# A hybrid attention and RWKV-7 block on one Trainium2 core: the second half's first RWKV head pair placed after the first half's attention in the program text

## The chip, the cores and the metric

The kernel runs on one core of a Trainium2 chip. What counts is the device time of one execution in microseconds, from the first instruction to the last; for the kernel before it is given as the median of three runs. The engines are called by the names that the profile uses: PE is TensorE's matmul stream, PEld its weight loads, DVE is VectorE, ACT is ScalarE, POOL is GpSimd and SP is SyncE, which issues most of the DMAs.

## The reference, cut to what matters

The block takes a sequence of 1024 frames with 1024 features. One combined projection feeds two groups of heads side by side, sparse attention and RWKV-7 time mixing; their outputs are concatenated and projected back, and an FFN follows. Everything is fp32.

```python
h = rms_norm(x, g_mix) * (1 + sc1) + sh1
proj = h @ w_in                                    # columns: attention part, RWKV part
o_a = dsa_attention(q, rms_norm(c_lat, g_kv), q_idx, k_idx, w_idx, ...)
o_b = rwkv7_time_mix(token_shift(p_b, mu_shift), ...)
x = x + gt1 * (concat(o_a, o_b) @ w_out)
h = rms_norm(x, g_ffn) * (1 + sc2) + sh2
u = relu(h @ w_ff1)
x = x + gt2 * ((u * u) @ w_ff2)

# dsa_attention, for each block of 128 queries:
rel = relu(einsum('bthd,bsd->bths', qi, k_idx))
score = einsum('bth,bths->bts', wi, rel)           # the indexer, 8 heads
_, sel = top_k(where(key < limit, score, -inf), 256)
# softmax attention over the selected keys only, with a linear distance penalty

# rwkv7_time_mix, 8 heads of 64, one step per frame:
sa = einsum('bhij,bhj->bhi', state, -kk_t)
state = state * w_t + sa[..., None] * (kk_t * a_t) + v_t[..., None] * k_t
out_t = einsum('bhij,bhj->bhi', state, r_t)
```

## The kernel before, in words

**Halves.** The sequence is cut into two halves of 512 frames. For each half the kernel runs, in this order of the text: the norm; the RWKV projections (`rwkv_proj`); for the first half the RWKV time mixing (`rwkv`) and then the attention projections (`attn_proj`), the indexer with its selection of 256 keys (`indexer`) and the attention itself (`attention`); then the output projection (`out_proj`) with a second norm (`norm_T`), and the FFN (`ffn`). The two halves are woven together: the second half's RWKV projections stand behind the first half's indexer, and the second half's indexer and attention are started from inside the FFN of the first half.

**Dense products.** An fp32 product is made of three matmuls (`dense`): each weight tile `wraw` is split on the chip into a high part `whi` (cast on ACT, L399) and a rest `wlo` (subtraction on POOL or DVE), each activation into `hh` and `hl`. One block of 128 output columns with 1024 inputs is 24 matmuls of 512 columns into a PSUM bank `ps_mm`. In what follows "dense matmuls" are these.

**The selection.** The indexer sums 8 heads of scores (matmuls `ps_f<-kiH,iqs` and `ps_f<-kiL,iqs`, relu on ACT, sums `sc` on DVE at L897). A bisection over 32 bits then finds each query's 256th largest score: counts on ACT (`jka`, L931) and on DVE, and a few tiny DVE steps for each bit. Its last DVE steps (L979 to L986) make the masks `mk`.

**Attention.** `attention` runs over four head pairs. For each it loads the keys `kr`, splits them (`kh` on ACT at L1007, `klo` on DVE at L1008) and the queries (`qs`, `q`), and for each 128 queries makes the scores (`ps_f<-kh,qs`, `ps_f<-klo,q`, `ps_f<-conb,nsl`), adds the mask with a running maximum (L1039), takes the exponential, transposes (`ps_c<-con,L`) and multiplies by the values (`ps_o<-PT,vj`).

**RWKV.** The time mixing works on head pairs j = 0 to 3 (two heads of 64 on the 128 partitions) and on chunks of 64 frames. For a pair, `rwkv_feat` makes the decay, the key and the receptance features (matmuls `ps_f<-w2a,tw`, `ps_f<-xa,a2w`, `ps_f<-con,sig`, then `gram` with `ps_f<-KR,Bh`, masked into `Lb`); `rwkv_feat1` adds `rk`, `bvs` and `BKs`. `rwkv_inv` then inverts eight triangular 64x64 matrices: copies `Ld` (L633) and a transpose `Lu`, 15 steps of substitution on DVE (L652, L655) on 32x32 blocks, transposes `D` and `AT`, four rounds of small matmuls (`ps_f<-AT,Lc`, `ps_f<-D,Gs`, `ps_f<-AT,Lb`, `ps_f<-D,Gs`), and a copy into `TT` (L700). `rwkv_feat2` prepares more operands, and `rwkv_chain` runs the eight chunks one after the other: `Xb`, a product with `TT`, `Ub`, the state update `H` (L725) and the output `On`. `rwkv_out` normalizes `On` (square, power on POOL, transposes `ps_c<-con,On` at L747, a gate product `ps_c<-sg,g2w`) and stores it.

In the loop of `rwkv`, the inverse of pair j+1 is written ahead of the chain of pair j and ends behind it, and the features of pair j+2 follow:

```python
        setup(0)
        for u in (0, 4):
            rwkv_feat2(hf, 0, R[0], u)
        R[1] = rwkv_feat(hf, 1, L4, rp, bp)
        rwkv_feat1(hf, 1, R[1], rp, bp)
        for j in range(4):
```

`rwkv_head` is what stands ahead of that loop: it loads three low-rank inputs (`tw`, `xa`, `sg`) and runs `rwkv_feat`, the whole `rwkv_inv` and `rwkv_feat1` of pair 0. Its results go to `rwkv` as L4 and R0.

**What sets the order.** A scheduler places the instructions of each engine in one fixed order. It starts from the order of the program text as a priority, and lets an instruction go ahead of an earlier one that has to wait, by its own estimates. Tiles limit it: a tile can be written only when the tile that had its buffer before has been read for the last time, and the buffers of a tag are handed out in program order. PSUM has eight banks of 512 columns, by tag: `mm` 2, `dx` 1, `f` 2, `c` 2, `o` 1. The RWKV features and inverses, the attention scores and the indexer's products all use the two banks of `f`. On the chip each engine then runs its order strictly, and waits where an operand is not there.

Of the kernel before, what the change touches and what calls it, by code (L numbers as in the profile page):

```python
# [111 lines left out]
def body(tc, I, out, dbg=None):  # L112
# [359 lines left out]
    def rwkv_proj(hf, hT):  # L472

        mark('bproj%d' % hf)
        GRP[0] = 2 * hf
        sl = slice(hf * HALF, hf * HALF + HALF)
        pss = pst("dx")
        for i in PO:
            if i == 0:
                y = shifted(hf, hT, 0, 1536)  # L480
                A.activation(y[0:64], y[0:64], AF.Tanh)
                held.append((xwd[:, sl], y))
                y = shifted(hf, hT, 1, 1664)
                sigmoid(y, y)
                held.append((sgd[:, sl], y))
            for j in range(4):
                y = shifted(hf, hT, 2 + i * 4 + j, i * 512 + j * 128)
                held.append((rkvd[i * 4 + j, :, sl], y))
                if i == 1:
                    sq = dp.tile([128, HALF], F32, name="fsq", tag="fsq", bufs=2)  # L490
                    A.activation(sq, y, AF.Square, scale=P("k_k", j, j + 1))
                    stat(pss, sq, j)
            if i == 1:
                inverse(pss, 0, sl, None, 1e-24)
        release()
# [73 lines left out]
    def rwkv_feat1(hf, j, R, rp, bp):  # L569

        mark('feat%d%d' % (hf, j))
        sl = slice(hf * HALF, hf * HALF + HALF)
        v2 = rp.tile([128, 8, 64], F32, name="v2", tag="v2", bufs=1)
        nc.sync.dma_start(v2, c3(rkvd[8 + j, :, sl]))
        bvs = (bp if j % 3 else rp).tile([128, HALF], F32, name="bvs", tag=f"bvs{j % 3}", bufs=1)
        Bh, Kh, WC = R["Bh"], R["Kh"], R["WC"]
        BKs = rp.tile([128, 8, 2, 64], F32, name="BKs", tag="BKs", bufs=1)
        wcb = WC.unsqueeze(2).to_broadcast([128, 8, 64])
        EN(4).tensor_tensor(BKs[:, :, 0, :], c3(Bh), wcb, ALU.mult)
        EN(5).tensor_tensor(BKs[:, :, 1, :], c3(Kh), wcb, ALU.mult)  # L580
        rk = rp.tile([128, HALF], F32, name="rk", tag="kap", bufs=1)
        V.scalar_tensor_tensor(rk, R["rT"], P("r_k", j, j + 1), R["kp"], ALU.mult, ALU.mult)
        pb = pst("f")
        slow[hf, j] = mmul(pb, C("oblk"), rk)
        V.tensor_tensor(c3(bvs), c3(pb), v2, ALU.mult)
        R.update(bvs=bvs, BKs=BKs, v2=v2)
# [572 lines left out]
    def rwkv_head(hf, rp):  # L1159
        sl = slice(hf * HALF, hf * HALF + HALF)  # L1160
        tw = rp.tile([65, HALF], F32, name="tw", tag="tw", bufs=1)
        xa = rp.tile([128, HALF], F32, name="xa", tag="xa", bufs=1)
        sg = rp.tile([128, HALF], F32, name="sg", tag="sg", bufs=1)
        G.memset(tw[64:65], 1.0)
        nc.sync.dma_start(tw[0:64], xwd[0:64, sl])
        nc.sync.dma_start(xa, xwd[:, sl])
        nc.sync.dma_start(sg, sgd[:, sl])
        L4 = (tw, xa, sg)
        R0 = rwkv_feat(hf, 0, L4, rp, None)
        R0["TT"] = TT0  # L1170
        for _ in rwkv_inv(hf, 0, R0, rp):
            pass
        rwkv_feat1(hf, 0, R0, rp, None)
        return L4, R0
# [47 lines left out]
    def pool(name, side="left"):  # L1222
        cm = tc.tile_pool(name=name, bufs=1, reuse_waits="tile", side=side)
        return cm, cm.__enter__()

    def done(cm):
        cm.__exit__(None, None, None)
# [8 lines left out]
    rp_cm, rp = pool("rp")  # L1236
# [12 lines left out]
    masks = indexer(0, ix, mk)  # L1249
    done(ix_cm)  # L1250
    rwkv_proj(1, hT1)
    head1 = rwkv_head(1, rp)
    at_cm, at = pool("at0")
    for _ in attention(0, masks, at):
        pass
    done(at_cm)
    done(mk_cm)
    done(nx_cm)
    fp_cm, fp = pool("ff0", "right")
    small["ff0"] = fp  # L1260
# [99 lines left out]
```

## Time and profile before

| | |
|---|---|
| median of three runs | 1782.17 us |
| lowest and highest of them | 1781.13 and 1788.82 us |
| the profiled execution, its own time | 1785.96 us |
| its span (first to last instruction) | 1784.2 us |
| mean granted clock of TensorE | 0.972 |

The profile is of one execution, which took a little longer than the median; times inside it are counted from its first instruction. Its stages of interest, read from its timeline: the first half's bisection ends at 503 us, the head of the second half runs from 481 to 531 us beside it, the first half's attention from 531 to 601 us, the second half's four chains from 617 to 785 us, the output projection of the first half and its norm to 830 us, the second half's indexer to 889 us and its bisection to 1035 us. From 1238 us on there are hardly any but FFN matmuls.

### The profile page before, as it was taken

How to read it: one execution, taken by the hardware profiler on the slowest of the kernel's cores; microseconds unless marked ns; L12 is line 12 of the kernel's file. 1: busy time of each engine (PE TensorE's matmuls, PEld its weight loads, DVE VectorE, ACT ScalarE, POOL GpSimd, SP SyncE). 2: the span in 40 equal slices, each digit the busy share in tenths (PEclk: the TensorE clock that was granted, in tenths of full speed). 3: DMA queues.
4: the chain of work that ended last, by engine and by line, in shares of the span. 5: the costliest groups of instructions: out<-in, count | busy, mean ns of one | idle time of the engine just before them, and what ended most of it. 6: DMA issues, size and time to landing. Idle time of an engine off the chain costs nothing. (4 is left out here: it accounts for less than half of the span.)

```text
span 1784.2 us, 27312 instructions
## 1 busy us (share of the span) xinstructions
PE 1616.8 (91%) x9380; PEld 1217.4 (68%) x9380; DVE 1047.8 (59%) x2701; ACT 878.1 (49%) x1840; POOL 565.8 (32%) x751
## 2 busy tenths in 40 slices
PE   5997888988879988899968899999999999999998
PEld 2776655666655566666646676777886788888887
DVE  3786578559877676646999558763114233333333
ACT  3334364555637654535755865765235252525251
POOL 2555334353451344153224454113554300000000
PEclk9998999999999999999979999999999999999999
DMA  8895234333443441322112234324332333333332
GB/s 298 275 302 152 79 103 137 123 106 105 136 114 100 151 146 60 107 65 71 54 42 83 65 101 118 95 72 151 104 96 70 115 116 95 100 95 94 95 98 79
DMA packets 264018, 203.90 MB, mean 114 GB/s; under 512 B 17300, under 2 KB 218004, under 8 KB 263879
## 3 DMA queue, kind: packets, MB, share of 16 engines
q1 hardware_dynamic: 253122, 182.90, 34.1%
q10 hardware_dynamic: 10628, 19.24, 2.9%
q8 instruction: 74, 1.21, 0.3%
q14 instruction: 66, 0.53, 0.1%
q0 software_dynamic: 128, 0.01, 0.0%
HBM read 173.32 MB, written 28.78 MB: 113 GB/s over the span
## 5 line engine op out<-in xcount | busy, mean ns | idle before, releaser
L136 POOL TENSOR_TENSOR wlo<-wraw,whi 128x256 fp32r<-128x256 f32 x512 | 404.4, 813 | 590.7 <-ACT whi L399 493.2
L121 PE MATMUL ps_mm<-hh,whi 128*128 128x512 f32 (+1 forms) x1024 | 420.1, 411 | 27.2 <-ACT whi L399 7.1
L399 ACT CAST whi<-wraw 128x512 fp32r<-128x512 f32 x384 | 235.6, 616 | 423.9 <-PE ps_mm L121 385.9
L121 PE MATMUL ps_mm<-hl,whi 128*128 128x512 f32 (+1 forms) x1024 | 419.1, 409 | 4.2 <-DVE hl L345 1.9
L121 PE MATMUL ps_mm<-hh,wlo 128*128 128x512 f32 (+1 forms) x1024 | 414.2, 405 | 0.1
L121 PEld LDWEIGHTS ps_mm<-hh,whi 128*128 128x128 f32 (+1 forms) x1024 | 195.7, 192 | 75.0 <-ACT whi L399 16.7
L121 PEld LDWEIGHTS ps_mm<-hl,whi 128*128 128x128 f32 (+1 forms) x1024 | 196.7, 192 | 48.9 <-issue 6.8
L121 PEld LDWEIGHTS ps_mm<-hh,wlo 128*128 128x128 f32 (+1 forms) x1024 | 196.2, 192 | 42.8 <-issue 4.7
L121 PE MATMUL ps_mm<-uh,whi 128*128 128x512 f32 x512 | 204.9, 400 | 16.4 <-ACT whi L399 6.3
L121 PE MATMUL ps_mm<-ul,whi 128*128 128x512 f32 x512 | 204.4, 399 | 6.1 <-DVE ul L1134 6.1
L121 PE MATMUL ps_mm<-uh,wlo 128*128 128x512 f32 x512 | 203.9, 398 | 0.2
L401 DVE TENSOR_TENSOR wlo<-wraw,whi 128x512 fp32r<-128x512 f32 x128 | 88.2, 689 | 130.0 <-ACT whi L399 128.9
L931 ACT ACTIVATE jka<-sc,canda 128x1024 bf16<-128x1024 f32 (+1 forms) x93 | 90.2, 970 | 77.4 <-DVE canda L929 52.2
L121 PEld LDWEIGHTS ps_mm<-uh,whi 128*128 128x128 f32 x512 | 97.5, 191 | 43.1 <-issue 11.4
L121 PEld LDWEIGHTS ps_mm<-ul,whi 128*128 128x128 f32 x512 | 97.8, 191 | 28.9 <-DVE ul L1134 7.3
L121 PEld LDWEIGHTS ps_mm<-uh,wlo 128*128 128x128 f32 x512 | 97.6, 191 | 23.9 <-POOL wlo L136 1.7
L1140 DVE SCALAR_TENSOR_TENSOR xT<-ps_mm,mod,xT 128x512 f32<-128x512 f32 x64 | 47.8, 748 | 109.7 <-PE ps_mm L121 109.7
L1134 DVE TENSOR_TENSOR ul<-ur,uh 128x512 fp32r<-128x512 f32 x64 | 44.6, 697 | 80.1 <-ACT uh L1133 80.1
L1039 DVE CUSTOM_DVE_ANT_0 L<-ps_f,mk 128x512 f32<-128x512 f32 (+3 forms) x96 | 51.6, 551 | 26.6 <-PE ps_f L121 13.2
L1045 ACT ACTIVATE L<-L,m 128x128 f32<-128x128 f32 (+7 forms) x64 | 49.6, 776 | 19.5 <-DVE m L1042 14.4
L720 ACT COPY Ub<-ps_c 64x64 f32<-64x64 f32 x128 | 26.3, 205 | 65.5 <-DVE UV L718 56.9
L291 DVE SCALAR_TENSOR_TENSOR macc<-mraw,cs,macc 128x512 f32<-128x512 f32 x56 | 49.9, 890 | 10.0 <-DMA mraw<-in_w_ada_dram 8.5
(329 smaller groups left out, 2602.0 us busy)
## 6 DMA issues: line engine op xcount, KB each, us to landing
wraw<-in_w_ff_dram SPq DMA_DIRECT2D x256, 256.0 KB
wraw<-in_w_in_dram SPq DMA_DIRECT2D x92, 256.0 KB
mraw<-in_w_ada_dram SPq DMA_DIRECT2D x64, 256.0 KB
mraw<-in_w_ada_dram SPq DMA_DIRECT2D x16, 512.0 KB
wraw<-in_w_out_dram SPq DMA_DIRECT2D x32, 256.0 KB
rkvd<-shy ACTq DMA_DIRECT2D x24, 256.0 KB
xin<-in_x_dram SPq DMA_DIRECT2D x8, 512.0 KB
rt<-rnd SPq DMA_DIRECT2D x32, 128.0 KB
```

Of the source, the lines that this page charges most:

```text
L121: r = T.matmul(out, lhsT, rhs, start=start, stop=stop, **kw)
L136: G.tensor_tensor(o[:, c], a[:, c], b[:, c], op)
L291: V.scalar_tensor_tensor(acc, raw, c, acc, ALU.mult, ALU.add)
L399: (A.copy if HE[GRP[0]] == "a" else V.tensor_copy)(hi[:, :, 0:M], raw[:, :, 0:M])
L401: (V if LE[GRP[0]] == "v" or LE[GRP[0]] == "m" and GRP[1] else InHalves).tensor_tensor(lo[:, :, 0:M], raw[:, :, 0:M], hi[:, :, 0:M].bitcas ...
L720: (V.tensor_copy if CE[2] == "v" else A.copy)(Ub[h * 64:h * 64 + 64, h, :], pu[u, h * 64:h * 64 + 64])
L931: A.activation(jka[:, 0:width(b)], sc[b], AF.Sign, scale=-1.0, bias=0.0 if bit == 31 else canda.bitcast(F32)[:, i:i + 1], accum_out=ca[:, ...
L1039: V.tensor_tensor_reduce(L[:, c0:c0 + n], ps[:, 0:n], masks[b][:, c0:c0 + n], 1.0, -3e38, ALU.add, ALU.max, m2[:, pc:pc + 1])
L1045: A.activation(L[:, 0:W], L[:, 0:W], AF.Exp, bias=m2[:, 2:3], accum_out=m2[:, 3:4])
L1134: V.tensor_tensor(b, r, a.bitcast(F32), ALU.subtract)
L1140: V.scalar_tensor_tensor(xT[:, d, :], ps, mod[:, 40 + d:41 + d], xT[:, d, :], ALU.mult, ALU.add)
```

## The change

One line moves. The call of `rwkv_head` for the second half stood between the second half's RWKV projections and the first half's attention; now it stands behind that attention and the release of its pools.

```diff
--- before.py
+++ after.py
@@ -1249,12 +1249,12 @@
     masks = indexer(0, ix, mk)
     done(ix_cm)
     rwkv_proj(1, hT1)
-    head1 = rwkv_head(1, rp)
     at_cm, at = pool("at0")
     for _ in attention(0, masks, at):
         pass
     done(at_cm)
     done(mk_cm)
+    head1 = rwkv_head(1, rp)
     done(nx_cm)
     fp_cm, fp = pool("ff0", "right")
     small["ff0"] = fp
```

As the scheduler starts from the text, and as banks are handed out by it, the move shows in the order of each engine. Up to the first matmul of the head the PE order is the same in both kernels, and again from a place that lies at 1238 us of the profile before. The head's loads and the DVE product `kap` keep their early place; the rest of it moves.

On DVE, at the end of the first half's bisection, the kernel before has the steps that make the last mask (`eq`, `jk`, `mk_3932`) mixed with feature steps of the head (`Bh`, `rk`, `Lb`) and followed by the start of its inverse (`Ld`, `Lu`):

```order
L564 SCALAR_TENSOR_TENSOR Bh<-at,wrec 128x512
L983 SCALAR_TENSOR_TENSOR sc_3944<-eq,zer 128x512
L582 SCALAR_TENSOR_TENSOR rk<-rT,prm,kp 128x512
L984 SCALAR_TENSOR_TENSOR eq<-sc_3944,need,eq 128x512
L597 TENSOR_TENSOR Lb<-ps_f,conb 128x512
L985 TENSOR_TENSOR jk<-jk,eq 128x512
L597 TENSOR_TENSOR Lb<-ps_f,conb 128x512
L986 TENSOR_SCALAR mk_3932<-jk 128x512
L633 COPY Ld<-Lb 32x256 x2
L1016 TENSOR_SCALAR q_5316<-ones_82 1x512
L636 STREAM_TRANSPOSE Lu<-Ld 128x1024
```

In the changed kernel the mask's steps stand alone, and attention's own preparations follow at once:

```order
L983 SCALAR_TENSOR_TENSOR sc_3944<-eq,zer 128x512
L984 SCALAR_TENSOR_TENSOR eq<-sc_3944,need,eq 128x512
L985 TENSOR_TENSOR jk<-jk,eq 128x512
L986 TENSOR_SCALAR mk_3932<-jk 128x512
L1016 TENSOR_SCALAR q_5066<-ones_82 1x512
L1016 TENSOR_SCALAR q_5067<-ones_82 1x512
L1008 TENSOR_TENSOR klo_5064<-kr,kh_5075 64x512
L1014 TENSOR_TENSOR qs_5080<-qr,qs_5080 64x512
L1015 CAST q_5066<-qs_5080 64x512
L1014 TENSOR_TENSOR qs_5093<-qr,qs_5093 64x512
L1015 CAST q_5067<-qs_5093 64x512
```

The feature steps and the start of the inverse have left this place, and the mask and the first attention steps have closed up.

On PE, the second place is the end of the inverse of pair 0. In the kernel before it is followed by the first scores of attention:

```order
L121 MATMUL ps_mm<-hh,whi 128x512
L121 MATMUL ps_f<-D,Gs 32x32 x16
L121 MATMUL ps_f<-rk,con 128x512
L121 MATMUL ps_f<-kh_5325,qs_5330 128x128
L121 MATMUL ps_f<-klo_5314,q_5316 128x128
L121 LDWEIGHTS nsl
L121 MATMUL ps_f<-conb,nsl 128x128
```

In the changed kernel the features' `w2a` of pair 0 stands behind the last scores of attention, where the `w2a` of pair 1 stood, and the inverse of pair 0 is followed by the `w2a` of pair 1 and the first step of pair 0's chain (`Xb`, `TT`):

```order
L121 MATMUL ps_mm<-hh,wlo 128x512
L121 MATMUL ps_f<-D,Gs 32x32 x16
L121 MATMUL ps_f<-rk,con 128x512
L121 MATMUL ps_f<-w2a,tw 128x128 x4
L121 MATMUL ps_f<-xa,a2w 128x512
L121 MATMUL ps_c<-Xb_6067,TT_1310 128x128
L121 MATMUL ps_mm<-hh,whi 128x512
L121 MATMUL ps_f<-con,sig 128x128 x4
L121 MATMUL ps_c<-UV,BKn 128x128
```

So the inverse's end has moved from ahead of attention to behind it, and the features of pair 1 from the end of attention to the end of that inverse. The `w2a` of pair 2 stands behind the eighth chunk of pair 0's chain, where it stood between the sixth and the seventh; that of pair 3 behind the sixth chunk of pair 1's chain, where it stood behind the seventh.

The third place on PE is the norm behind the output projection. Between the last chain's last state product and this norm stand 96 dense matmuls in the kernel before and 38 in the changed one, of which 10 behind the last transposes of `On`. In the kernel before, products of the second half's indexer (`kiH`, `kiL`) stand inside the norm (`sq`, `part`):

```order
L121 MATMUL ps_mm<-hh,wlo 128x512
L121 MATMUL ps_dx<-sq,ones_82 32x512 x2
L121 MATMUL ps_f<-kiH,iqs 128x512
L121 MATMUL ps_f<-kiL,iqs 128x512
L121 MATMUL ps_f<-kiH,iqs 128x128
L121 MATMUL ps_f<-kiL,iqs 128x128
L121 MATMUL ps_dx<-sq,ones_82 32x512 x4
L121 MATMUL ps_f<-kiH,iqs 128x512
L121 MATMUL ps_f<-kiL,iqs 128x512
L121 MATMUL ps_f<-kiH,iqs 128x256
L121 MATMUL ps_f<-kiL,iqs 128x256
L121 MATMUL ps_dx<-sq,ones_82 32x512 x2
```

In the changed kernel the norm stands alone, and the first indexer products come behind the fourteenth dense matmul of the FFN:

```order
L121 MATMUL ps_mm<-hh,wlo 128x512
L121 MATMUL ps_dx<-sq,ones_82 32x512 x8
L374 MATMUL ps_dx<-con,part 128x128 x4
L121 MATMUL ps_dx<-con,r_8696 128x128 x4
L121 MATMUL ps_mm<-hh,whi 128x512 x2
L121 MATMUL ps_mm<-hl,whi 128x512
```

Twelve pairs of indexer products have moved from inside the norm to behind it.

## Rows read from the trace of the kernel before

**Rows 1.** The page: busy us (share of span) and instructions by engine.

```profile
PE 1616.8 (91%) x9380; PEld 1217.4 (68%) x9380; DVE 1047.8 (59%) x2701; ACT 878.1 (49%) x1840; POOL 565.8 (32%) x751
```

**Rows 2.** Windows: length; busy us of PE, PEld, DVE, ACT, POOL; granted clock.

```profile
481.00:531.00 50.00, 37.22 (x341) 26.84 (x341) 38.06 (x97) 21.76 (x45) 28.43 (x39) 0.90 0.43 123
...
617.00:785.00 168.00, 150.38 (x1385) 109.75 (x1386) 112.07 (x344) 80.28 (x223) 60.22 (x83) 0.97 0.30 96
...
830.00:889.00 59.00, 55.18 (x227) 38.06 (x228) 57.92 (x92) 42.41 (x88) 18.70 (x18) 1.00 0.16 48
```

**Rows 3.** PE's waits, 480 to 531 us: total, times, longest.

```profile
PE ps_f L121 <- DVE AT L661: 4.1, 1, 4.1
PE ps_f L121 <- POOL sig L199: 3.2, 1, 3.2
PE ps_dx L121 <- ACT asq L769: 2.8, 2, 2.4
PE ps_f L121 <- DVE Bh L564: 2.7, 1, 2.7
```

**Rows 4.** A short window, same columns.

```profile
484.00:492.00 8.00, 4.78 (x19) 3.65 (x18) 6.64 (x24) 6.81 (x15) 5.14 (x7) 0.79 0.36 101
```

**Rows 5.** ACT timeline: start, duration, instruction [idle before <- releaser].

```profile
510.37 0.62 ACT L1007 CAST kh<-kr 128x512 fp32r<-128x512 f32 x1 [2.45 <-DMA kr<-khd]
...
529.72 0.74 ACT L700 COPY TT<-ps_f 32x256 f32<-32x256 f32 x2 [0.32 <-PE ps_f L121]
```

**Rows 6.** DVE timeline: first copy of pair 0's inverse, first masked sum.

```profile
503.75 1.57 DVE L633 COPY Ld<-Lb 32x256 f32<-32x256 f32 x2
...
531.39 0.28 DVE L1039 CUSTOM_DVE_ANT_0 L<-ps_f,mk 128x128 f32<-128x128 f32 x1
```

**Rows 7.** PE timeline: start of the features of pairs 1, 2, 3.

```profile
596.16 1.16 PE L121 MATMUL ps_f<-w2a,tw 65*128 65x128 f32 x8
...
645.72 0.71 PE L121 MATMUL ps_f<-w2a,tw 65*128 65x128 f32 x4
...
692.68 0.71 PE L121 MATMUL ps_f<-w2a,tw 65*128 65x128 f32 x4
```

**Rows 8.** DVE timeline: rt, and the inverses' first copies (pairs 1, 2, 3).

```profile
602.71 1.15 DVE L782 SCALAR_TENSOR_TENSOR rt<-rt,gqk 128x512 f32<-128x512 f32 x1 [4.31 <-DMA rt<-rnd]
...
615.00 1.04 DVE L633 COPY Ld<-Lb 32x256 f32<-32x256 f32 x2
...
660.02 1.03 DVE L633 COPY Ld<-Lb 32x256 f32<-32x256 f32 x2
...
708.53 0.58 DVE L633 COPY Ld<-Lb 32x256 f32<-32x256 f32 x2
```

**Rows 9.** DVE timeline: first and eighth state update, last chain.

```profile
759.63 0.57 DVE L725 SCALAR_TENSOR_TENSOR H<-H,WC,ps_c 64x64 f32<-64x64 f32 x2
...
785.25 0.58 DVE L725 SCALAR_TENSOR_TENSOR H<-H,WC,ps_c 64x64 f32<-64x64 f32 x2
```

**Rows 10.** PE timeline: last On transposes, dense matmuls, norm, first FFN matmul.

```profile
796.58 1.26 PE L747 MATMUL ps_c<-con,On 128*128 128x128 f32 x4 [2.98 <-POOL On L136]
...
811.78 0.39 PE L121 MATMUL ps_mm<-hl,whi 128*128 128x512 f32 x1
...
815.41 0.39 PE L121 MATMUL ps_mm<-hh,wlo 128*128 128x512 f32 x1
815.73 1.05 PE L121 MATMUL ps_dx<-sq,ones 128*32 128x512 f32 x4
...
829.96 0.72 PE L121 MATMUL ps_mm<-hh,whi 128*128 128x512 f32 x2
```

**Rows 11.** PE by lines, 816 to 829.9 us: count | busy, mean ns.

```profile
L121 PE MATMUL ps_f<-kiH,iqs 128*128 128x512 f32 (+3 forms) x12 | 5.0, 413 | 0.4 <-ACT rl L893 0.2
L121 PE MATMUL ps_f<-kiL,iqs 128*128 128x512 f32 (+3 forms) x12 | 4.1, 358 | 0.0
```

**Rows 12.** DVE by lines, 830 to 889 us, same columns.

```profile
L897 DVE SCALAR_TENSOR_TENSOR sc<-rl,wn,sc 128x512 f32<-128x512 f32 (+3 forms) x56 | 38.4, 743 | 0.7 <-ACT rl L893 0.2
```

## The prediction

> **What bounds the kernel now.** I read the page first: TensorE (PE) is busy for 91% of the span, the next engine for 59% [rows 1]. So a change pays where PE stands still, or where something that PE waits for later comes earlier. The busy time by stretches shows where that can be [rows 2]. From 481 to 531 us, where the moved code runs now, PE is busy for 37.22 of 50 us at a granted clock of 0.90, and from 617 to 785 us, the four chains of the second half, for 150.38 of 168. From 830 to 889 us it is VectorE (DVE) that is busy, for 57.92 of 59 us: there the second indexer's sums set the pace and not PE. That is the frame: dense matmuls (the fp32 products made of three matmuls) fill every hole that they can reach in program order, and a serial thread (bisection, attention, head, chains, norm, indexer, bisection) runs through them.
>
> PE's waits from 480 to 531 us name four long ones, 12.8 us in all: AT of the inverse 4.1, sig 3.2, asq 2.8 and Bh 2.7 [rows 3]. Three of them belong to the head that is moved. After the wait for sig the clock was 0.79 from 484 to 492 us [rows 4], part of it at 1.2 and part at 2.4 GHz, so the matmuls behind a hole pay too.
>
> **The change, part by part.** Nothing is added or removed: the same instructions stand in another order, so every term is a shift.
>
> *Attention starts earlier.* Now the first masked sum (L1039) comes at 531.39 us, though the order has the step that ends the last mask directly ahead of the inverse's first copy, at 503.75 [rows 6]. Between them lie the inverse (its last copy to TT at 529.72) and attention's casts. The first cast of keys, at 510.37, waited for the DMA of kr [rows 5], which the change does not touch; so I put the new first sum at about 511 us, 20 us earlier. Bounds: 506, if the transfer comes sooner once SyncE's queue is shorter there, and 531, if nothing moves. Attention then needs what it needs now: from its first sum to the w2a of the features behind it, 531.39 to 596.16, 64.8 us [rows 6, 7]. So that place in PE's order is reached at 576 us.
>
> *The head comes behind it.* The order shows that head 1's w2a takes exactly the place that pair 1's features have now, and that these fall back behind the inverse of pair 0, because features, inverse and scores share two PSUM banks that are handed out in program order. So a fifth link enters a chain of links. Its price: w2a to Ld (features) is 14.3 us for pair 2 (645.72 to 660.02), 15.8 for pair 3 (692.68 to 708.53) and 18.8 for pair 1 (596.16 to 615.00), in which DVE waited 4.31 us for a DMA of rt; Ld to the next pair's w2a (the inverse) is 30.7 us (615.00 to 645.72) and 32.7 (660.02 to 692.68) beside a running chain [rows 7, 8], and 26.0 for pair 0, which had no chain beside it (503.75 to 529.72) [rows 5, 6]. With 14.3 and 26.0, as no chain runs there in the new order either: 576 + 14.3 + 26.0 + 14.3 = 630.6 us for pair 1's Ld, which now stands at 615.00. That is 15.6 us late. The loop over the later pairs is the same in both, but for one thing: pair 3's w2a stands behind the sixth update of pair 1's chain where it now stands behind the seventh. One update is 3.7 us long (the last chain's eight: 759.63 to 785.25 in seven steps [rows 9]); this gives back between 0 and 3.7, and I take 2. The last chain then ends 13.6 us late, at 799 us. Bounds: 576 + 18.8 + 30.7 + 18.8 = 644.3, 29 late, with the dear rows; or 3 late, if features without a chain beside them take 12 and the inverse 20 (estimates below the nearest rows, 14.3 and 26.0).
>
> *PE is further on when that chain ends.* What PE loses in holes and at the low clock before 531 us goes to dense matmuls. The order gives the amount: behind the last chain's last update stand 96 dense matmuls before the norm now, and 38 in the changed kernel. 58 fewer at 0.227 us (16 steps from 811.78 to 815.41 [rows 10]) are 13.2 us. Is the gate behind the chain late then? The transposes of On come 11.3 us after the last H (785.25 to 796.58), because squares, power and a GpSimd product stand between [rows 9, 10]. 28 dense matmuls (6.4 us) lie before them in the new order, so PE waits about 4 us there, as it waits 2.98 now; 10 lie behind, at half speed 4.5 us, with the transposes and the gate product some 2. That makes 17.8 us from the last H to the norm, and 30.5 - 13.2 = 17.3 by the count (815.73 - 785.25 = 30.5): the two agree. The norm starts at 13.6 - 13.2 = +0.4 us.
>
> *The norm and the second indexer.* In the 14.2 us from the norm's first matmul to the first FFN matmul (815.73 to 829.96) PE now runs 12 pairs of indexer products (kiH, kiL) inside the norm's waits [rows 10, 11]. In the new order they stand behind the fourteenth FFN matmul. The norm alone gets a little faster: between 0 and 4.2 us (9,472 columns of the pairs at 0.227 us for 512, if all of it lay in its path); I take 0.9, as most of them stand where PE would wait for squares. The pairs lose their cover: they cost the same 4.2 us if they run as densely as the dense matmuls, and 9.1 by the two rows' busy time not overlapped (5.0 + 4.1). I take 5.3, near the dense end, since what they stream between is dense. Below, it is nothing if these pairs find other holes; above, 12 of DVE's sums at 743 ns are 8.9 us [rows 12], since that engine sets the pace up to the bisection.
>
> **The sum.** 13.6 - 13.2 - 0.9 + 5.3 = +4.8 us. The profiled execution took 1785.96 us (span 1784.2), 3.8 above the median of the three, 1782.17; as the shift counts against either, I put 1787 us on the median. About 0.5%, 8.9 us, is what a measurement can tell here from no change.
>
> The Trainium skill (Perfetto Trace Analysis, Optimization Strategy) says that a kernel whose most contended engine changes over time may gain by interleaving such regimes. This change takes a latency-bound head out of the bisection and sets it in front of other latency-bound links, so the rule speaks against it. The same section reads a repeated bubble as a possible lack of buffers for the next tile; two shared PSUM banks would be such a place, and no trace here has more of them.
>
> **Rivals.** *Slower by more than 0.5%: the links add up to more.* Place: between the end of attention and pair 1's Ld. By the dear rows the last chain ends 27 us late and the sum is 27 - 13.2 - 0.9 + 5.3 = +18, 1800 us; halfway, at 20 late, it is +11, 1793. For it: pair 1's features took 18.8 us at this very place, DVE waiting for rt, and the clock was low after each hole. Against: no chain's copies queue between the steps of pair 0's inverse. It decides from 17.7 us late on (8.9 + 13.2 + 0.9 - 5.3), only 4.1 above my value. By the Trainium skill's sentence on interleaving, cited above, the time would come out here.
>
> *Faster by more than 0.5%: the link hides.* Attention ends 20 us sooner, features and inverse without a chain cost 12 and 20 us, the last chain ends 3 late and the pairs are hidden: 3 - 13.2 - 0.9 + 0 = -11, 1771 us. For it: PE's 12.8 us of waits and the low clock go from a place where nothing else could run. Against: both link times lie below every row. It decides from 5 us late on, and only with the pairs hidden.
>
> *The change does not do what it says.* The head's loads and the product for kap keep their early place by the order; were the features to run early too, the sum would be nothing, 1782. The order speaks against it, and the case lies within 0.5%.
>
> **How the numbers follow.** Forecast, with the last rival, 0.48 (about 1780 to 1790); slower rival 0.35; faster rival 0.17. The range reaches from the faster rival to the slower one's end, leaving out the dearest mixtures: 1772 to 1802. The forecast's own range is 1779 to 1791.
>
> **What would show it.** In the changed kernel's trace: the first L1039 at about 511 us; w2a of the head at 576; pair 0's Ld at 590 and pair 1's at 631; the last H update at 799; the norm's first matmul at 816, the first FFN matmul at 829.5; the end of the second indexer's sums, and with it the second bisection, some 5 us later; from about 1240 us on the same order, shifted by the sum. I am wrong if attention does not start before 520 us; if pair 1's Ld comes after 635 us or before 622; if the last H and the norm do not move together by 13 us less; or if the second bisection starts earlier than now.

## The result, and the profile after

| | before | changed |
|---|---|---|
| median, four runs each | 1781.91 us | 1798.25 us |
| lowest and highest | 1781.13 to 1788.82 | 1796.57 to 1800.55 |
| profiled execution, its own time and span | 1785.96, 1784.2 | 1796.80, 1795.0 |
| ratio, 95% interval | | 1.0084 (1.0055 to 1.0112) |

The change makes the kernel slower by 0.84%, some 15 us. In a later session the same two kernels gave 1.0076 (1.0063 to 1.0089). My likeliest case, within 0.5%, did not hold; the first rival, slower by more than that, did. The time lies inside the range (1772 to 1802), near its upper end, and the sum of +4.8 us was about a third of the shift.

The two profiled executions are 10.8 us apart in span, and both spend alike up to 460 us. What I read next is the busy time by stretches, cut at the same events in both kernels: first masked sum of the first half's attention, last masked sum, last state update, first FFN matmul, first count of the second bisection, last masked sum of the second half's attention, end. The columns are the length, then busy us of PE, PEld, DVE, ACT, POOL, the granted clock, DMA share and GB/s. First the kernel before:

```profile
460.00:531.40 71.40, 54.36 (x414) 40.28 (x412) 54.33 (x170) 35.88 (x77) 37.09 (x51) 0.93 0.44 126
531.40:595.50 64.10, 59.64 (x357) 37.36 (x358) 49.13 (x200) 45.23 (x122) 4.50 (x6) 0.97 0.34 104
595.50:785.30 189.80, 169.48 (x1534) 123.17 (x1533) 122.86 (x368) 95.04 (x257) 72.00 (x103) 0.96 0.34 107
785.30:830.00 44.70, 40.40 (x161) 26.82 (x159) 17.80 (x35) 18.86 (x36) 21.69 (x26) 0.92 0.31 89
830.00:888.70 58.70, 54.88 (x226) 37.80 (x227) 57.62 (x92) 42.11 (x88) 18.70 (x18) 1.00 0.16 47
888.70:1210.30 321.60, 282.81 (x1533) 216.44 (x1532) 243.44 (x686) 207.38 (x388) 110.54 (x135) 0.96 0.28 81
1210.30:1784.20 573.90, 563.60 (x2522) 454.45 (x2520) 185.56 (x274) 220.32 (x369) 96.89 (x131) 1.00 0.34 102
```

Then the changed kernel:

```profile
460.00:506.60 46.60, 37.85 (x147) 28.93 (x148) 35.00 (x121) 26.23 (x56) 21.75 (x28) 0.93 0.48 139
506.60:578.90 72.30, 67.11 (x381) 41.38 (x380) 50.48 (x202) 49.29 (x129) 8.94 (x11) 0.97 0.40 122
578.90:804.60 225.70, 198.24 (x1831) 145.13 (x1829) 139.28 (x412) 102.69 (x274) 91.54 (x130) 0.93 0.30 97
804.60:836.50 31.90, 21.23 (x80) 11.97 (x80) 9.11 (x21) 11.46 (x20) 12.76 (x16) 0.92 0.27 77
836.50:902.30 65.80, 63.16 (x256) 43.53 (x257) 63.67 (x103) 48.38 (x102) 17.13 (x19) 0.96 0.16 49
902.30:1225.80 323.50, 284.28 (x1520) 214.22 (x1520) 244.02 (x685) 207.24 (x389) 111.48 (x138) 0.96 0.28 81
1225.80:1795.00 569.20, 561.13 (x2529) 452.62 (x2525) 185.31 (x274) 218.31 (x365) 94.37 (x127) 1.00 0.34 102
```

What PE lost in a stretch I estimate as its length less busy time times clock. Before, the seven come to 20.8, 6.2, 27.1, 7.5, 3.8, 50.1 and 10.3 us; after, to 11.4, 7.2, 41.3, 12.4, 5.2, 50.6 and 8.1. The sums are 125.8 and 136.2: the 10.4 us between them are nearly the 10.8 of the spans. That they come so near is in part luck: the clock is given to 0.01, and half of that is 2.8 us over the 563.60 us of the last stretch. The larger differences still show where the time went. Ahead of attention PE gained 9.4 us, which the change was able to give. In the stretch from attention to the last chain's end it lost 14.2 more, and from there to the FFN 4.9 more. All that follows together differs by 0.3 us in these rows, which the rounding of the clock makes uncertain by some 3.

The links behind attention, in the changed kernel's timeline of DVE (start, duration, instruction, in brackets the idle time before it and what ended it; `Ld` begins an inverse, `H` is a state update):

```profile
506.55 0.27 DVE L1039 CUSTOM_DVE_ANT_0 L<-ps_f,mk 128x128 f32<-128x128 f32 x1
...
594.30 1.86 DVE L633 COPY Ld<-Lb 32x256 f32<-32x256 f32 x2
...
621.80 0.57 DVE L725 SCALAR_TENSOR_TENSOR H<-H,WC,ps_c 64x64 f32<-64x64 f32 x2 [1.36 <-PE ps_c L121]
...
631.21 0.69 DVE L597 TENSOR_TENSOR Lb<-ps_f,conb 128x512 f32<-128x512 f32 x1 [1.01 <-PE ps_f L121]
631.93 0.53 DVE L633 COPY Ld<-Lb 32x256 f32<-32x256 f32 x1
...
637.48 0.53 DVE L725 SCALAR_TENSOR_TENSOR H<-H,WC,ps_c 64x64 f32<-64x64 f32 x2
...
680.27 0.58 DVE L633 COPY Ld<-Lb 32x256 f32<-32x256 f32 x2
...
728.66 0.57 DVE L633 COPY Ld<-Lb 32x256 f32<-32x256 f32 x2
...
804.63 0.59 DVE L725 SCALAR_TENSOR_TENSOR H<-H,WC,ps_c 64x64 f32<-64x64 f32 x2 [0.63 <-PE ps_c L121]
```

And in its timeline of PE:

```profile
578.58 0.94 PE L121 MATMUL ps_f<-w2a,tw 65*128 65x128 f32 x6
...
617.83 1.09 PE L121 MATMUL ps_f<-w2a,tw 65*128 65x128 f32 x8
...
627.48 3.68 PE L121 MATMUL ps_f<-KR,Bh 64*64 64x128 f32 x32 [2.77 <-DVE Bh L564]
...
632.96 0.63 PE L121 MATMUL ps_o<-Vbd,Mt 128*128 128x128 f32 x2
...
663.99 1.16 PE L121 MATMUL ps_f<-w2a,tw 65*128 65x128 f32 x8
...
675.82 3.68 PE L121 MATMUL ps_f<-KR,Bh 64*64 64x128 f32 x32 [4.64 <-DVE Bh L564]
...
710.57 0.49 PE L121 MATMUL ps_f<-w2a,tw 65*128 65x128 f32 x2
...
817.43 1.26 PE L747 MATMUL ps_c<-con,On 128*128 128x128 f32 x4 [4.66 <-POOL On L136]
...
823.06 1.05 PE L121 MATMUL ps_dx<-sq,ones 128*32 128x512 f32 x4
...
836.53 1.22 PE L121 MATMUL ps_mm<-hh,whi 128*128 128x512 f32 x2 [2.56 <-ACT hh L388]
```

The matmuls with pair 2's `Bh`, which took 3.68 us here, in the PE timeline of the kernel before:

```profile
654.77 1.96 PE L121 MATMUL ps_f<-KR,Bh 64*64 64x128 f32 x32 [1.27 <-DVE Bh L564]
```

Against [rows 6 to 10]: the first masked sum came 24.8 us earlier; the last state update came 19.4 us later (804.63 against 785.25), the norm 7.3 and the first FFN matmul 6.6. Then the second bisection, by the first count on ACT, before and after:

```profile
888.69 0.95 ACT L931 ACTIVATE jka<-sc 128x896 bf16<-128x896 f32 x1 [1.71 <-DVE sc L900]
```

```profile
902.25 0.95 ACT L931 ACTIVATE jka<-sc 128x896 bf16<-128x896 f32 x1
```

It starts 13.6 us later, 7.0 more than the first FFN matmul, and 2.8 of these 13.6 were given back by the end.

### The profile page after: what moved, and what is told of

It is laid out like the page before. It is cut to its first block, busy times and chain, and to the rows that moved or that the text cites. A ratio compares the mean times of both kernels' runs of the same rounds, so it can differ in the third digit from the quotient of the medians.

```text
span 1795.0 us, 27302 instructions
## 1 busy us (share of the span) xinstructions
PE 1620.9 (90%) x9380; PEld 1214.4 (68%) x9380; DVE 1043.9 (58%) x2701; ACT 876.1 (49%) x1840; POOL 561.4 (31%) x751
## 5 line engine op out<-in xcount | busy, mean ns | idle before, releaser
L121 PE MATMUL ps_mm<-uh,whi 128*128 128x512 f32 x512 | 203.5, 398 | 15.7 <-DVE xT L1140 5.0
L1134 DVE TENSOR_TENSOR ul<-ur,uh 128x512 fp32r<-128x512 f32 x64 | 44.2, 690 | 79.6 <-ACT uh L1133 79.6
L121 PE MATMUL ps_o<-PT,vj 128*64 128x128 f32 x576 | 51.0, 280 | 4.5 <-DMA vj<-vd 3.5
```

Of the source, the lines that this page charges most:

```text
L121: r = T.matmul(out, lhsT, rhs, start=start, stop=stop, **kw)
L1134: V.tensor_tensor(b, r, a.bitcast(F32), ALU.subtract)
```

## The experiments

Three theories were held against each other. **A**: the head is one more link in the serial row behind attention (features, inverse, features, inverse, chain), which PE cannot fill, so that the late chain end outweighs PE's lead. **B**: the head is dear there for its engines' own sake, whatever the PSUM banks. **C**, later **R**: the link does not matter, but the place of the dense matmuls and of the second indexer's pairs does. Each ratio below is to the kernel before on the same chip, with its 95% interval.

The times in the table are from one profiled execution each; the part up to 460 us, which is the same in all, differs by some us between executions (the changed kernel has its w2a at 617.8 in one and at 622.5 in the other), so that small differences say nothing.

| run | ratio | pair 1's w2a | last state update |
|---|---|---|---|
| changed kernel, again | 1.0076 (1.0063 to 1.0089) | 622.5 | 808.3 |
| inverse on other banks | 1.0035 (1.0016 to 1.0055) | 595.9 | 799.3 |
| head cut in two | 1.0059 (1.0036 to 1.0082) | 599.5 | 793.7 |
| changed, early indexer | 1.0199 (1.0181 to 1.0217) | 617.4 | 803.1 |
| before, early indexer | 1.0122 (1.0103 to 1.0141) | 596.8 | 787.3 |
| changed, link shortened | 0.9984 (0.9970 to 0.9998) | 604.0 | 779.3 |
| before, link shortened | 1.0001 (0.9981 to 1.0022) | 586.3 | 784.9 |
| before, pairs behind the norm | 1.0015 (1.0002 to 1.0027) | 601.0 | 787.9 |
| head behind 1st pair of attention | 1.0006 (0.9994 to 1.0019) | 616.5 | 804.3 |
| head behind 2nd pair | 0.9955 (0.9938 to 0.9971) | 606.7 | 790.4 |
| head behind 2nd pair, again | 0.9970 (0.9956 to 0.9984) | 610.6 | 796.5 |
| head behind 3rd pair | 1.0011 (0.9997 to 1.0025) | 610.7 | 799.8 |

**The inverse on other banks.** The inverse of the second half's pair 0 takes its banks from another tag:

```diff
-    head1 = rwkv_head(1, rp)
+    head1 = rwkv_head2(1, *rwkv_head(1, rp), rp, "c")   # rwkv_head: features; rwkv_head2: inverse, with its tag, and feat1
```

> The changed kernel, with one difference: the inverse of the second half's pair 0 takes its four PSUM banks from the tag c instead of f, so that pair 1's features no longer have to wait behind it (their w2a then stands right behind the last values product of attention). Theory A (the loss comes from pair 1's features queueing behind pair 0's inverse on the two f banks, so that the last chain ends 19.4 us later while PE is only 12.1 us ahead): pair 1's first Ld copy at 612 to 620 us instead of 631.9, the last H update at 788 to 796 instead of 804.6, time 1784 to 1791 us. Theory B (features and inverse are slow there for their engines' own sake, whatever the banks): first Ld copy within 3 us of 631.9, time 1795 to 1800. Theory C (the chain's end does not matter, the indexer's pairs behind the norm do): the Ld may move, the time stays at 1794 to 1800, because eleven of the twelve pairs are still behind the norm.

About half of the loss is gone (0.35% are left of 0.76 to 0.84), within A's time; A's `Ld` and last update were missed. Its PE timeline shows pair 1's features early, and they run beside the inverse:

```profile
595.89 1.05 PE L121 MATMUL ps_f<-w2a,tw 65*128 65x128 f32 x8
...
609.61 3.68 PE L121 MATMUL ps_f<-KR,Bh 64*64 64x128 f32 x32 [5.25 <-DVE Bh L564]
...
626.76 0.69 PE L121 MATMUL ps_c<-D,Gs 32*32 32x32 f32 x30
```

Its DVE timeline shows why that gave so little:

```profile
613.34 0.69 DVE L597 TENSOR_TENSOR Lb<-ps_f,conb 128x512 f32<-128x512 f32 x1 [0.31 <-PE ps_f L121]
...
627.56 0.58 DVE L633 COPY Ld<-Lb 32x256 f32<-32x256 f32 x2 [3.06 <-PE ps_c L121]
```

Pair 1's `Lb` is begun at 613.34, 18 us earlier than in the changed kernel (631.21 there), yet the first copy `Ld` comes at 627.56, only 4.4 us earlier, and it waited 3.06 us for PE. The matmuls that begin at 626.76 and end just ahead of that copy are the last of pair 0's inverse. The tile `Ld` has one buffer, which the inverse's `Gs` also uses: by the program the second inverse cannot begin before the first has done its last reads of it. The first inverse also took longer beside the features, 31 us (`Ld` at 596.24) for 23.5 in the changed kernel. So theory A's banks explain the queue that the features stood in, and the row of links stays, inverse behind inverse; what a second buffer for `Ld` would give was not run. B missed too: its bound was 3 us and its time 1795 to 1800, 1.007 to 1.010.

**The head cut in two.** Features ahead of attention, inverse behind it:

```diff
     head1 = rwkv_head(1, rp)          # features alone
     ...
     done(mk_cm)
+    rwkv_head2(1, *head1, rp)         # inverse and feat1
     done(nx_cm)
```

> The head cut in two: pair 0's features stay ahead of attention as in the kernel before, its inverse and the rk, bvs and BKs part go behind attention. Theory A: the features leave the row of links behind attention but the inverse of 26 us stays in it, pair 1's w2a at about 600 to 606 us, the last H update at 788 to 795, time 1782 to 1789 us. Theory B: the same row of links with only the features' 15.7 us taken out, last H at 789 to 795. Theory C: the order has the twelve indexer pairs inside the norm again, so the whole loss is back, 1780 to 1784.

The links went as A said (w2a at 599.5, last update at 793.7), the time did not: its 1782 to 1789 us are ratios of 1.000 to 1.004, and 1.0059 lies above them (its interval begins at 1.0036). C is out as well: all twelve pairs ran inside the norm again, and most of the loss stayed. In this stretch, from attention's last sum to the last update, PE lost 43 us by the estimate above (205.5 - 182.62 x 0.89), against 27.1 before:

```profile
588.20:793.70 205.50, 182.62 (x1659) 132.44 (x1657) 125.45 (x369) 96.95 (x263) 72.31 (x104) 0.89 0.32 102
```

The norm came at 828.6, 35 us behind the last update, with 110 dense matmuls in between: here PE was the bound and not the chain. About half of these 43 us are clock (182.62 x 0.11 = 20), and 17.5 of them lie in one stretch at a granted clock of 0.50, 1.2 GHz, in which PE was busy all the same:

```profile
718.70:756.20 37.50, 35.03 (x295) 28.20 (x296) 15.55 (x57) 12.54 (x38) 1.39 (x3) 0.50 0.25 78
```

Without that stretch the loss here is some 23 us, less than in the whole one of the kernel before. Whether the order or the single execution brings that stretch is not known: the profiled one took 1802.0 us, 5.6 more than the median of this run.

**The early indexer.** The second half's indexer is started ahead of the output projection, in the changed kernel and in the kernel before:

```diff
-UI = 0
-UA = (UI,) * 5
+UI = -1
+UA = (0,) * 5
```

> The changed kernel, with the second half's indexer started in the text ahead of the output projection instead of inside the FFN, so that its twelve pairs stand inside and right behind the norm again; up to the norm PE's order is that of the changed kernel. Theory A: only the 5 to 7 us that the pairs cost behind the norm come back on the second bisection's start (902.25 us before this), time 1791 to 1796 us. Theory C: nearly all comes back, 1782 to 1787. If the pairs cost nothing: 1797 to 1800.

> The kernel before with the same edit (second indexer started ahead of the output projection in the text), as the control for the run above: twelve pairs from just ahead of the norm on instead of inside it. Theories A and C both expect little, 1779 to 1786 us: the pairs already run inside the norm there. A gain or loss beyond 4 us would mean that the edit itself does more than move the pairs, and the run above would have to be read against it.

All expectations missed, and the control did so by as much. In the changed kernel with this edit the second bisection starts at 885.39 us, 17 us earlier than without:

```profile
885.39 0.95 ACT L931 ACTIVATE jka<-sc 128x896 bf16<-128x896 f32 x1 [1.21 <-DVE sc L900]
```

Yet the time rose by more than 1%. So the start of the second bisection does not by itself decide the end. In the control the FFN's first matmul came at 874.2 us instead of 829.96, with DVE busy for 39.95 of the 44.2 us ahead of it and PE for 27.77:

```profile
830.00:874.20 44.20, 27.77 (x106) 16.36 (x105) 39.95 (x89) 29.84 (x62) 1.02 (x1) 0.91 0.02 7
```

DVE worked on the indexer while the FFN stood. For the pairs alone these two runs can't be read; but one ratio over the other is 1.0199 / 1.0122 = 1.0076, the loss of the change once more, with the pairs moved in both. That speaks against C.

**The link shortened.** Fifteen substitution steps of one inverse are left out:

```diff
-        for c in range(15, 0, -1):
+        for c in range(0 if (hf, j) == (1, 0) else 15, 0, -1):
```

> The changed kernel without the fifteen substitution steps of the inverse of the second half's pair 0 (its 32x32 blocks are left uninverted; everything else of the inverse is still done), so that this one link behind attention gets some 10 to 13 us shorter. Theory A (the time is lost because features and inverse of pair 0 now stand as one more link in the serial row behind attention, which PE cannot fill): pair 1's w2a at 604 to 608 us instead of 617.8, the last H update 8 to 13 us before 804.6, and most of the loss is back: ratio to the kernel before 0.996 to 1.004. Rival R (the loss lies in where the order puts the dense matmuls and the indexer's pairs, not in the link's length): the ratio stays at 1.006 to 1.010 although the link is shorter.

> The kernel before without the same fifteen steps, as the control. There the inverse runs beside the casts of attention, which wait for a DMA until 510 us anyway. Theory A: attention starts some 8 to 12 us earlier than 531.4, worth 3 to 8 us in the end, ratio 0.995 to 0.999. Rival R: no change, 0.998 to 1.002. The run above is read against this one: what leaving out the steps gives in both is the price of DVE's work, what it gives only there is the place's.

These two runs weigh most. In the changed kernel the inverse took 12.4 us for 23.5 (`Ld` at 591.63), so the link became 11.2 us shorter; pair 1's w2a came 13.8 us earlier (604.00 against 617.83), 2.6 of them from an earlier start. The ratio fell from 1.0084, or 1.0076, to 0.9984: the whole loss and a little more. In the kernel before, the same steps left out gave nothing that can be told, 1.0001 within some 4 us. So the work costs nothing measurable where it stood and some 16 to 18 us where it was put. A's 0.996 to 1.004 held for the first; for the control A expected a gain that did not come, and R's no change held. By the order 126 dense matmuls stand behind the control's last update, so PE may bound its norm; that is argued and not shown, as its profiled execution took 1797.5 us, 10.8 more than its median. From the timelines of PE and DVE with the link shortened:

```profile
604.00 1.09 PE L121 MATMUL ps_f<-w2a,tw 65*128 65x128 f32 x8
...
806.46 1.05 PE L121 MATMUL ps_dx<-sq,ones 128*32 128x512 f32 x4
```

```profile
779.27 0.59 DVE L725 SCALAR_TENSOR_TENSOR H<-H,WC,ps_c 64x64 f32<-64x64 f32 x2 [0.63 <-PE ps_c L121]
```

The last update came 25 us earlier (779.27 against 804.63), more than the link lost and more than A's 8 to 13. The order behind the link had changed with it: 80 dense matmuls stand behind the last update and not 38, and the indexer's pairs are inside the norm again. So the 16 to 18 us are those of the link and of what the scheduler makes of it, not of its length alone.

**The pairs behind the norm.** In the kernel before, the second indexer is started one block of the FFN later in the text (`UI` and with it `UA`, the place of the second attention, are 1 and not 0), and its first pair may not go ahead of a matmul of the FFN's first block, by an order-only dependency:

```diff
-UI = 0
+UI = 1
 ...
+tc.add_manual_dep(first.ins, dm[-18].ins.name, DependencyInfo(NoSync, DATA), reason="order")
```

> The kernel before with one thing of the changed kernel: the second indexer's pairs may not start before the FFN's thirteenth matmul (an order-only dependency), so that all twelve stand behind the norm as they do in the changed kernel; the head stays ahead of attention. This measures the term of 5.3 us by itself. Theory A (with the late chain, this is the second part of the loss): the second bisection starts 5 to 9 us after 888.7 and the ratio is 1.002 to 1.005. Rival R (the pairs' place carries most of the loss of 0.84%): 1.006 to 1.010. If the start of the second bisection does not decide the end, as the two runs with the early indexer suggest: 0.999 to 1.002.

The ratio, 1.0015, is some 2.7 us, within the last case's range and below A's; A's bisection start, 5 to 9 us late, held (6.3). In its trace thirteen FFN matmuls stand ahead of the first pair. Its PE timeline has the norm without pairs, its ACT timeline the bisection's start:

```profile
818.40 1.05 PE L121 MATMUL ps_dx<-sq,ones 128*32 128x512 f32 x4
...
831.87 0.73 PE L121 MATMUL ps_mm<-hh,whi 128*128 128x512 f32 x2 [2.55 <-ACT hh L388]
```

```profile
894.99 0.94 ACT L936 ACTIVATE jka<-sc 128x896 bf16<-128x896 f32 x1
```

The norm alone took 13.47 us, as in the changed kernel (823.06 to 836.53), and 14.23 before. From the norm's start to the bisection it was 76.6 us here, 73.0 before and 79.2 in the changed kernel. So the pairs' place costs about a fifth of the loss (0.15 of 0.76%, and by its interval at most 0.27); R, in which it carries most, is out.

**Other places for the head.** It is written behind the first, second or third of attention's four head pairs:

```diff
-    for _ in attention(0, masks, at):
-        pass
+    for n, _ in enumerate(attention(0, masks, at)):
+        if n == 1:                        # 0, 1, 2
+            head1 = rwkv_head(1, rp)
```

> The whole head written behind the first of attention's four head pairs instead of behind the fourth. Theory A: attention starts at 505 to 510 us as in the changed kernel, but features and inverse lie beside the second and third pair, so that nothing but pair 1's features stands behind attention, as in the kernel before; the last H update comes at 770 to 785 us and the ratio is 0.992 to 0.999. Rival R: by the order only 6 dense matmuls are left at the norm and the indexer's pairs stand behind the thirty-eighth FFN matmul, so PE runs dry at the norm and the ratio is 1.002 to 1.010.

> The whole head written behind the second of attention's head pairs. Theory A: as the run above with a little less room, pair 1's w2a behind attention's last products at 585 to 595 us, last H at 772 to 788, ratio 0.993 to 1.000. Rival R: 30 dense matmuls are left at the norm and the pairs stand behind the fourteenth FFN matmul as in the changed kernel, ratio 1.002 to 1.009.

> The whole head written behind the third of attention's four head pairs. Theory A: the inverse lies beside the last pair only, so part of the link sticks out behind attention: pair 1's w2a at 588 to 605 us, between the second place (606.7, with a longer attention) and the changed kernel (617.8), last H at 790 to 800, ratio 0.997 to 1.004. If the place hardly mattered and the second place had its gain from elsewhere: 1.005 to 1.010.

> The changed kernel once more, beside the other places on the same chip: 1.0055 to 1.0112 again, if the chip makes no difference.

> The head behind the second of attention's head pairs once more, beside the changed kernel on the same chip: 0.9938 to 0.9971 again, clear of no change.

Behind the second pair the kernel is faster than both, 0.9955 and 0.9970 in two sessions, and the changed kernel beside it gave 1.0076. In its timelines of PE and DVE:

```profile
540.31 1.05 PE L121 MATMUL ps_f<-w2a,tw 65*128 65x128 f32 x8
...
606.72 0.38 PE L121 MATMUL ps_f<-w2a,tw 65*128 65x128 f32 x2
...
802.02 1.26 PE L747 MATMUL ps_c<-con,On 128*128 128x128 f32 x4 [3.97 <-POOL On L136]
...
805.86 1.05 PE L121 MATMUL ps_dx<-sq,ones 128*32 128x512 f32 x4
```

```profile
790.41 0.59 DVE L725 SCALAR_TENSOR_TENSOR H<-H,WC,ps_c 64x64 f32<-64x64 f32 x2 [0.63 <-PE ps_c L121]
```

The head begins at 540.31, beside attention's third pair, and pair 1's w2a follows attention at 606.72 without an inverse between them. The last update is 5 us later than before, not earlier as A had it, and the norm starts 9.9 us earlier than before (805.86 against 815.73). The stretch from attention to that update runs at a clock of 0.99:

```profile
606.70:790.40 183.70, 166.28 (x1532) 121.81 (x1530) 118.18 (x346) 91.88 (x250) 74.25 (x107) 0.99 0.28 87
```

By the estimate above it lost 19.1 us (183.7 - 166.28 x 0.99), against 27.1 before and 41.3 in the changed kernel; the estimate closes less well here, as its seven stretches give 10.3 us less than before and the spans differ by 5.4 (1784.2 and 1778.8). The ratio is inside A's range, but A's w2a (585 to 595) and last update (772 to 788) were missed. R is out here too: 30 dense matmuls are left at the norm and the pairs stand behind the fourteenth FFN matmul, nearly as in the changed kernel, and the time is shorter. The first place missed both theories' ranges: the inverse lay beside attention, but attention took 107 us (509.2 to 616.5) and the dense matmuls were used up: none begins between 802.35 and 824.24 us, where the norm runs. The third place lies between the second and the changed kernel, as A had it, though its w2a came nearly 6 us later than A allowed.

## Why the prediction was right and wrong

*Attention starts earlier*: right, 506.55 us for 511, at the lower bound. It took longer, 72.0 us for 64.8, with 7.5 us more PE work in it, so that the head's w2a came at 578.58 for 576.

*The head comes behind it*: right in kind and nearly in size up to pair 1. Features 15.7 us for 14.3 (578.58 to 594.30), inverse 23.5 for 26.0 (594.30 to 617.83), the next features 14.1 for 14.3; pair 1's `Ld` at 631.93 for 630.6. What failed is the size of the step behind it, from there to the last update, which came 19.4 us late and not 13.6. I had called the later pairs the same in both kernels, but for 2 us that come back. These came back: pair 2's inverse took 30.3 us (680.27 to 710.57) for 32.7. What I had put at nothing did not stay the same: pair 1's inverse took 32.1 us for 30.7, pair 2's features 16.3 for 14.3 and pair 3's 18.1 for 15.8. With the 1.3 us up to pair 1's `Ld` that is 6.9 us, of which 1.1 came back on the way to the last update; 5.8 is the error. The two features took as long in the changed kernel's second profile (16.3 and 18.1), and 14.3 and 15.9 to 16.0 in two other profiles with the order of the kernel before up to the norm, so the order makes the difference and not the execution.

The rows above show it for pair 2: the matmuls behind `Bh` waited 4.64 us and took 3.68, before 1.27 and 1.96. Where it comes from is read from one trace: pair 0's second chunk stood in PE's order behind pair 1's `KR,Bh` and `rk`, so its update came at 637.48, 15.7 us behind the first (one chunk is 3.7 [rows 9]), and that chain ended at 663.3, just ahead of pair 2's w2a. Its output steps then stood on POOL from 667.50 to 670.92, ahead of the product for `at` that `Bh` waited for. The late second chunk alone is not the loss: it came 15.8 us behind the first with the link shortened too. Of the prediction's two bounds on the lateness, the 29 us are those of pair 1's `Ld`; for the last chain it is the 27 of the first rival.

*PE is further on*: right, 12.1 us (19.4 - 7.3) for 13.2. The wait for `On` was 4.66 us for 4.

*The norm and the pairs*: the norm gained 0.8 us for 0.9. The pairs were taken at 5.3 us; by themselves they cost 4.4 us up to the bisection (76.6 - 73.0 + 0.8) and some 2.7 in the time.

*The sum*: with the measured lateness my terms give 19.4 - 12.1 - 0.8 + 4.4 = 10.9 us, and the spans differ by 10.8. That is closer than the terms are: in the changed kernel itself the stretch from the first FFN matmul to the bisection grew by 7.0 us and not 4.4, and 2.8 were given back later. Against the medians, 15 to 16 us, some 4 to 6 us stay unexplained by the one profile of each. The last step of the argument, that the second bisection's start carries the shift to the end, is wrong as a mechanism: the early indexer moved it by 17 us and the end the other way. What reached the first FFN matmul, 6.6 us, is the chain's lateness less PE's lead; how the rest of the loss arises behind it is not shown.

The first rival had the outcome and the point from which it decides, 17.7 us late; 19.4 is beyond it. Its place, between attention's end and pair 1's `Ld`, was not where the excess arose: that `Ld` came 1.3 us behind my forecast. The Trainium skill's sentence on interleaving regimes (Perfetto Trace Analysis, Optimization Strategy) agrees with the runs here: the head's fifteen steps cost nothing measurable beside the bisection (1.0001 without them) and some 16 to 18 us behind attention. The Trainium skill's remark on buffers, in the same section, holds in part: with other banks about half of the loss was gone, and the second inverse of that run then waited for the first one's last matmuls.

Open stays why the clock stayed low for 37.5 us in the run with the head cut in two, and how much of the gain behind the second pair is the clock and how much the cover: no run separates these.

## What to carry to other kernels

A latency-bound piece costs what the engine beside it cannot fill: leave out a part of its work in both places, and the difference is the price of the place, with what the scheduler makes of it. When a piece is moved, set the lateness of the last link against the dense work that PE has done by then: here 19.4 us against 12.1, and behind the second pair 5.2 against 15.0; the difference is what reached the norm. Where a sum takes a loop as the same in both orders, check who now stands behind whom on each engine: here three steps that the sum had put at nothing took from 1 to 2 us more each, and that was most of its error up to the norm.

## What the runs showed of the hardware that was not expected

In the stretch from attention to the last state update the granted clock was 0.99, 0.96, 0.93 and 0.89 in four orders of nearly the same work, the first with the head behind attention's second pair, then before, changed, and cut in two. The second profiles of the first and the third gave 0.98 and 0.93 there. With some 170 to 200 us of PE work in it, that alone is from 2 to 20 us. In the rows here the low clock came with the long waits. In the changed kernel the 32 small matmuls behind the wait of 2.77 us for `Bh` took 3.68 us (627.48 above) at a granted clock of 0.50, 1.2 GHz, and so did those behind the wait of 4.64 us. The same 32 of pair 2 behind a wait of 0.98 us, in the kernel with the head behind the second pair, and those of pair 3 without a wait, in the changed kernel, took 1.96 at 1.00, 2.4 GHz:

```profile
666.40 1.96 PE L121 MATMUL ps_f<-KR,Bh 64*64 64x128 f32 x32 [0.98 <-DVE Bh L564]
```

```profile
721.79 1.96 PE L121 MATMUL ps_f<-KR,Bh 64*64 64x128 f32 x32
```
